# In chains of seven products, ScalarE copies one more partial sum out of PSUM, VectorE's lower add moves behind the fourth product, and the last due steps take no weight splits

## The chip, the cores and the metric

The kernel runs on one core of a Trainium2 chip. A core has TensorE (PE in the profile, with PEld for its weight loads), VectorE (DVE), ScalarE (ACT), GpSimd (POOL) and SyncE (SP), each with its own instruction stream, and DMA queues; engines wait for each other by semaphores. The metric is the device time of one execution in microseconds (us), the median over several runs.

## The reference

The reference is a decoder trunk of two layers on a sequence of 512 positions and 1024 features, in float32. Layer 0 mixes tokens by dilated sliding-window attention with 24 heads in three groups, layer 1 by a gated linear recurrence; each is followed by a gated FFN with a causal convolution of three taps. Cut to what the change touches:

```python
qkv = (x @ w_qkv).reshape(B, S, N_GROUPS, 3, HEADS_PER_GROUP, HEAD_DIM)

def causal_dwconv(x, w, b):
    K = w.shape[0]
    xp = jnp.pad(x, ((0, 0), (K - 1, 0), (0, 0)))
    out = b
    for k in range(K):
        out = out + xp[:, k:k + S] * w[k]
    return out

def conv_ffn(x, w_up, conv_w, conv_b, w_down):
    u = causal_dwconv(x @ w_up, conv_w, conv_b)
    g, v = u[..., :D_FF], u[..., D_FF:]
    return (jax.nn.gelu(g, approximate=True) * v) @ w_down
```

## The kernel before, in words

**Precision.** Each float32 operand is split into a high and a low part: ScalarE writes `whi` (L220), VectorE subtracts it from the raw value and writes `wlo` (L221). A product is then three passes of TensorE, hi by hi, hi by lo and lo by hi (`PASSES`). The weights come by DMA into `raw`, and for the chains GpSimd's queue adds blocks of them to each other by accumulating DMAs (L257); VectorE forms one of the sums itself (L283).

**Chains.** The first projection of both FFNs and the q and k projections of two head groups are done in chains: two 256-row halves of the weights by two 256-column halves of the activations in seven products instead of eight, with sums and differences of weight blocks (`LEFT`) and of activation blocks (`T`). One product is 12 matmuls of 128x256 (4 blocks by 3 passes, L1184). A chain uses two PSUM banks of 128x512. In `y[1]`, the left half gathers products 1, 6, 7 and 4 one upon another. In `y[0]`, the right half gathers products 5 and 3, and the left half is product 2. Two SBUF tiles `t[0]` and `t[1]` (named `part`) take copies by ScalarE: product 1, the sum of 1 and 6, and product 5 (L1193). After product 3, VectorE adds `t[0]` to `y[0]`, which completes the chain's upper result (L1197), and calls `top`. After product 7, VectorE writes the right half of `y[1]`, the sum of 1, 6 and 7 plus the copy of 5 (L1202); after product 4 the bank is the lower result, and `bottom` is called.

There are 56 chains: 16 in attention (`quad` weights) and 20 in each FFN (function `seven`, for `j` in 2 to 11, two halves each). In attention, `top` and `bottom` are one VectorE multiply each, from the bank to SBUF. In an FFN they are `begin`: ScalarE writes `u` from the whole bank with one tap's weight and the bias (L885; for lower results with negated weights, `neg`), VectorE adds the two other taps (L889, two instructions), then ScalarE applies gelu (L909) or VectorE multiplies with the gate (L913).

**What sets the order.** The order is written out by hand, and each engine works through its own list. `steps` gives each product a number: in an FFN chain `n` starts at 10 n (`CYCLE`) with its products at the offsets `AT` (1: 0, 5: 1, 2: 2, 6: 4, 3: 5, 7: 8, 4: 13), so that product 4 runs in the middle of the next chain; free numbers are filled with the second projection (`acc` matmuls, L493). TensorE's order in the middle of the stage is so 1, 5, 2, 4 of the chain before, 6, 3, fill, fill, 7. `slot` runs a step, then the functions that came due (`later(1, f)`: behind the next step), then `tick`, which pumps weight splits: at most `HALVES` = 14 split halves may be live. While `state["hold"]` is set, `tick` pumps none. Behind the last numbered step `seven` empties the list of due functions, one slot each.

Of the kernel before, what the change touches and what calls it, by code (L numbers as in the profile page):

```python
# [14 lines left out]
AF = mybir.ActivationFunctionType  # L15
ALU = mybir.AluOpType
# [118 lines left out]
def kernel(  # L135
# [25 lines left out]
    nc = tc.nc  # L161
# [19 lines left out]
    def nm(s):  # L181
        uid[0] += 1
        return f"{s}{uid[0]}"
# [18 lines left out]
    def new_last():  # L202
        return up_.tile([P, 2 * D + EVEN], F32R, tag="sum", name=nm("last"))
# [15 lines left out]
    def split(hi, lo, raw):  # L219
        nc.scalar.activation(hi, raw, AF.Copy)  # L220
        nc.vector.tensor_tensor(lo, raw, hi.bitcast(F32), op=ALU.subtract)  # L221

    plan = []
    state = {"dma": 0, "cv": 0, "used": 0, "live": 0, "next": 0, "hold": False, "even": False, "quiet": False, "still": False}
# [122 lines left out]
    def refill():  # L347

        i = state["cv"]
        if i >= state["dma"]:  # L350
            return
        if plan[i][0] == "quad":
            pieces.extend(strided_stream(i))
            state["cv"] += 24
            return
        if plan[i][0] == "seven":
            n = 1
            while plan[i + n][0] == "seven":
                n += 1
            pieces.extend(stream(i, n))  # L360
            state["cv"] += n
        else:
            if plan[i + 1 : i + 2] and plan[i + 1][0] == "seven":
                pieces.append((None, lambda: ahead(i + 1)))
            parts = parts_of(plan[i][0], raws[i])
            pieces.extend(plain(i, j, r, j == len(parts) - 1) for j, r in enumerate(parts))
            state["cv"] += 1

    def beside(key):
        return plan[key[0]][4:] and key[1] == 1  # L370

    def single(name):
        return (name[0] if isinstance(name, tuple) else name) in HALF

    def pump(limit=2):

        for _ in range(limit):
            if not pieces:
                refill()
            while pieces and pieces[0][0] is None:  # L380
                pieces.pop(0)[1]()
            if not pieces or pieces[0][0][0] >= state["dma"]:
                continue
            spare = beside(pieces[0][0])
            if spare and state["even"]:
                continue
            if spare or state["live"] + 2 - single(pieces[0][0][1]) <= HALVES:
                key, cuts, last = pieces.pop(0)
                cuts = cuts()
                his, los = [], []  # L390
                if spare:
                    t = new_last()[:, EVEN:].rearrange("p (a b o c) -> p a b o c", a=2, b=2, o=1)
                for n, raw in enumerate(cuts):
                    if spare:
                        hi, lo = t[:, 0, n], t[:, 1, n]
                    else:
                        hi, lo = (
                            wp.tile([P] + list(raw.shape[1:]), F32R, tag=t, name=nm("w" + t)) for t in ("hi", "lo")
                        )
                    split(hi, lo, raw)  # L400
                    his.append(hi)
                    los.append(lo)
                units[key] = (his, los)
                state["live"] += len(cuts) * (not spare)
                state["used"] += last
                while pieces and pieces[0][0] is None:
                    pieces.pop(0)[1]()
            while not state["quiet"] and state["dma"] < len(plan) and state["dma"] - state["used"] < RAW_BUFS:
                load()

    def load():
        i = state["dma"]
        kind, kd, cols, srcs = plan[i][:4]
        raw = wp.tile([P, kd, cols], F32, tag="raw", name=nm("raw"), bufs=RAW_BUFS)
        at = 0
        for src, n in srcs:
            nc.sync.dma_start(raw[:, :, at : at + n] if kind == "value" else raw[:, at : at + n, :], src)
            at += n
        raws[i] = raw
        state["dma"] += 1  # L420
# [13 lines left out]
    def done(n=2):  # L434
        state["live"] -= n
# [6 lines left out]
    def later(n, f):  # L442
        due.append([n, f])

    def slot(emit, length=1):
        emit()
        for d in list(due):
            d[0] -= 1
            if d[0] < 0:
                due.remove(d)  # L450
                d[1]()
        tick(length)
# [4 lines left out]
    def tick(length=1):  # L457
        for s in list(sides):
            s[0] -= length
            if s[0] <= 0:  # L460
                try:
                    s[0] = next(s[1])
                except StopIteration:
                    sides.remove(s)
        if not (state["hold"] or state["still"]):
            pump(1 if state["even"] or state["live"] >= HALVES - 4 else 2)
# [704 lines left out]
    def chain(right, top, bottom):  # L1171

        i = chunk()
        y, t = {}, []

        def step(n):
            W = take(i, LEFT[n][0])
            b, at = {1: (1, 0), 6: (1, 0), 7: (1, 0), 4: (1, 0), 5: (0, 256), 3: (0, 256), 2: (0, 0)}[n]
            if b not in y:
                y[b] = psum()  # L1180
            dst = y[b][:, at : at + 256]
            for k in range(4):
                for q, (wa, ha) in enumerate(PASSES):
                    mm(  # L1184
                        dst, W[wa][0][:, k, :], right[n](ha, k), start=n in (1, 5) and k == q == 0,
                        stop=k == 3 and q == 2, skip_group_check=True,
                    )
            done(1)
            if n == 1:
                t.extend(gen(s="part") for _ in range(2))  # L1190
            if n in (1, 5, 6):
                to = {1: t[0][:, 0:256], 6: t[0][:, 256:512], 5: t[1][:, 0:256]}[n]
                later(1, lambda: nc.scalar.activation(to, dst, AF.Copy))  # L1193
            elif n == 3:

                def upper():
                    nc.vector.tensor_tensor(y[0], y[0], t[0], op=ALU.add)  # L1197
                    top(y[0])

                later(1, upper)  # L1200
            elif n == 7:
                later(1, lambda: nc.vector.tensor_tensor(y[1][:, 256:512], dst, t[1][:, 0:256], op=ALU.add))  # L1202
            elif n == 4:
                later(1, lambda: bottom(y[1]))

        return lambda n: lambda: step(n)

    def seven(hT, T, begin, last, prep):

        right = rights(hT, T)  # L1210
        i0, acc, ends_at = state["next"], {}, CYCLE * 2 * len(SEVEN)

        def finish(b, ps, j, minus=False):
            later(2, begin(b, ps, j, minus, True))

        def ends(j, half):
            return (
                lambda ps: later(0, lambda: finish(2 * half, ps, j)),
                lambda ps: finish(2 * half + 1, ps, j, True),
            )  # L1220

        def rows(k, pair):
            W, A = take(i0, ("rows", k)), take(i0, ("act", k))
            for t in pair:
                if t not in acc:
                    acc[t] = psum("acc")
                mm3(acc[t], [a[0][:, of_tile(t)] for a in A], [two(w[0]) for w in W], not k, False)
            if pair[-1] == 3:
                done(2)

        fill = quarters(last, 1, hT, lambda ps: finish(3, ps, SEVEN[0] - 1))
        fill += [lambda k=k, p=p: rows(k, p) for k in range(REST[0]) for p in ((0, 1), (2, 3))]
        steps = {}
        n = 0
        for j in SEVEN:
            for half in range(2):
                f = chain(right, *ends(j, half))
                steps.update((CYCLE * n + AT[p], f(p)) for p in AT)
                n += 1
        free = free_slots(n)  # L1240
        assert len(free) == len(fill)
        steps.update(zip(free, fill))
        state["even"] = True
        for m in range(max(steps) + 1):
            if m == ends_at + 1:
                prep()
            if m in steps:
                slot(steps[m])
                if m > 2 * CYCLE and m % 5 == 0 and state["live"] < HALVES - 2:
                    pump(1)  # L1250
        while due:
            slot(lambda: None)
        state["even"] = False
        return acc

# [622 lines left out]
```

## Time and profile before

| | |
|---|---|
| median of 3 runs | 1365.1 us (1363.44 to 1367.1) |
| profiled execution | 1369.2 us, span 1367.4 us |
| PE busy over the span | 1338.2 us (98%) |
| VectorE busy over the span | 1103.7 us (81%) |
| ScalarE busy over the span | 807.7 us (59%) |
| first FFN's middle, 557 to 749 us | PE 192.00, VectorE 170.06, ScalarE 128.66 of 192 us |
| second FFN's middle, 1077 to 1269 us | PE 192.00, VectorE 170.05, ScalarE 128.76 of 192 us |
| attention's chains, 150 to 444 us | PE 287.69, VectorE 236.59, ScalarE 152.21 of 294 us |

A row of a timeline gives the start and the length in us, the engine, the line, the operation, output<-input by the program's names, the shape and the count of a run of like instructions, and in brackets the time that the engine was idle before it and what ended this. A row of a group gives line, engine, operation, names and count, then busy us, mean ns of one, and idle time before with its releaser.

### The profile page before, as it was taken

Reading aid. Unit: us, or ns where it says so; the run is one execution under the profiler, and the core shown is the slowest. Engines: PE = TensorE matmul, PEld = TensorE weight load, DVE = VectorE, ACT = ScalarE, POOL = GpSimd, SP = SyncE. Lnnn points to the kernel's source line nnn. Section 1 sums busy time; section 2 is a strip of 40 time slices with the busy share of each in tenths; the row PEclk is TensorE's granted clock in tenths of the full one; section 3 lists DMA queues with packets and bytes.
Section 4 is the critical chain, followed back from the end, with each engine's and each line's share of the span. In section 5 each row is a group of like instructions: output and inputs, shape, how many; then the busy total and the mean of one; then the engine's idle time right before and its main releaser. Section 6 shows DMA issues by size and latency. Waiting matters only on the chain.

```text
span 1367.4 us, 24126 instructions
## 1 busy us (share of the span) xinstructions
PE 1338.2 (98%) x8981; PEld 1255.3 (92%) x8981; DVE 1103.7 (81%) x2173; ACT 807.7 (59%) x1690; POOL 236.4 (17%) x392
## 2 busy tenths in 40 slices
PE   9999999999999999999999999999999999999997
PEld 7888999889899999999999889978899999999996
DVE  6686888887876899988888759768899988888853
ACT  7343555454546476666666646489576667666641
POOL 0341341212120102221221002000102222221000
PEclk9999999999999999999999999999999999999999
DMA  7553454747483647777775542431446777776411
GB/s 231 184 148 123 124 188 122 214 109 227 120 243 99 263 155 155 183 179 175 169 169 146 174 164 81 151 109 54 162 149 148 178 182 181 178 181 163 165 68 62
DMA packets 70638, 214.53 MB, mean 157 GB/s; under 512 B 10816, under 2 KB 14360, under 8 KB 58744
## 3 DMA queue, kind: packets, MB, share of 16 engines
q1 hardware_dynamic: 42552, 153.34, 33.2%
q0 software_dynamic: 27120, 58.60, 21.2%
q8 instruction: 70, 1.15, 0.3%
q10 hardware_dynamic: 848, 1.05, 0.2%
q14 instruction: 48, 0.39, 0.1%
HBM read 193.99 MB, written 18.96 MB: 156 GB/s over the span
## 4 chain that ended last, share of the span: by engine, by line
PE 62%; issue 19%; DVE 11%; DMA 5%; ACT 3%; POOL 0%; DVEq 0%; POOLq 0%; ACTq 0%; SPq 0%
PE ps L1184 31%; PE acc L493 16%; PE ps L493 6%; PE v L1381 6%; DVE wlo L221 4%; DMA raw<-in_attn_w_qkv_dram 2%; DVE u L889 1%; DMA raw<-in_ffn_w_up_dram 1%; PE v L1319 1%; PE S L1527 1%; ACT whi L220 1%; DMA ft<-turned 1%; PE S L1475 1%; PE O L493 1%; DVE ps L1197 0%
## 5 line engine op out<-in xcount | busy, mean ns | idle before, releaser
L221 DVE TENSOR_TENSOR wlo<-raw,whi 128x512 fp32r<-128x512 f32 x628 | 417.4, 686 | 94.8 <-ACT whi L220 94.1
L220 ACT ACTIVATE whi<-raw 128x512 fp32r<-128x512 f32 x628 | 370.8, 624 | 153.1 <-PE acc L493 43.5
L1184 PE MATMUL ps<-T,whi 128*128 128x256 f32 x1344 | 235.6, 276 | 0.3
L1184 PE MATMUL ps<-hT,whi 128*128 128x256 f32 x1344 | 235.0, 276 | 0.0
L493 PE MATMUL ps<-hT,whi 128*128 128x512 f32 (+1 forms) x928 | 223.8, 334 | 0.2 <-ACT whi L220 0.2
L1184 PEld LDWEIGHTS ps<-T,whi 128*128 128x128 f32 x1344 | 207.4, 191 | 2.9 <-ACT part L1193 0.7
L1184 PEld LDWEIGHTS ps<-hT,whi 128*128 128x128 f32 x1344 | 204.3, 191 | 0.7 <-ACT part L1193 0.2
L1184 PE MATMUL ps<-T,wlo 128*128 128x256 f32 x672 | 185.3, 276 | 0.0
L1184 PE MATMUL ps<-hT,wlo 128*128 128x256 f32 x672 | 185.1, 275 | 0.0
L493 PEld LDWEIGHTS ps<-hT,whi 128*128 128x128 f32 x928 | 159.7, 190 | 13.9 <-ACT whi L220 0.4
L257 POOL DMA_DIRECT2D raw<-in_ffn_w_up_dram x120 | 104.2, 950 | 391.8 <-DVE wlo L221 308.8
L493 PE MATMUL ps<-hT,wlo 128*128 128x512 f32 (+1 forms) x464 | 154.3, 333 | 0.4 <-DVE wlo L221 0.4
L493 PE MATMUL acc<-whi,ahi 128*128 128x512 f32 x336 | 128.0, 381 | 1.8 <-DVE u L889 1.8
L493 PE MATMUL acc<-whi,alo 128*128 128x512 f32 x336 | 127.7, 380 | 1.7 <-DVE alo L221 1.6
L1184 PEld LDWEIGHTS ps<-T,wlo 128*128 128x128 f32 x672 | 128.2, 191 | 0.0
L1184 PEld LDWEIGHTS ps<-hT,wlo 128*128 128x128 f32 x672 | 128.2, 191 | 0.0
L493 PE MATMUL acc<-wlo,ahi 128*128 128x512 f32 x336 | 127.3, 379 | 0.0
L1193 ACT ACTIVATE part<-ps 128x256 f32<-128x256 f32 x168 | 63.9, 380 | 76.7 <-PE ps L1184 73.9
L1381 PE MATMUL v<-whi,hT 128*128 128x512 f32 x320 | 102.7, 384 | 0.0
L493 PEld LDWEIGHTS ps<-hT,wlo 128*128 128x128 f32 x464 | 88.3, 190 | 7.5 <-DVE wlo L221 0.6
L1184 PE MATMUL ps<-last,whi 128*128 128x256 f32 x448 | 79.5, 278 | 6.5 <-DVE ps L1202 6.5
L889 DVE SCALAR_TENSOR_TENSOR u<-ps,cols,u 128x511 f32<-128x511 f32 x112 | 83.5, 746 | 2.0
(227 smaller groups left out, 2453.3 us busy)
## 6 DMA issues: line engine op xcount, KB each, us to landing
raw<-in_ffn_w_up_dram SPq DMA_DIRECT2D x48, 1024.0 KB
raw<-in_attn_w_qkv_dram SPq DMA_DIRECT2D x34, 1024.0 KB
raw<-in_ffn_w_up_dram POOLq DMA_DIRECT2D x120, 256.0 KB, 5.6
raw<-in_ffn_w_down_dram SPq DMA_DIRECT2D x14, 1024.0 KB
dw<-in_ffn_w_down_dram SPq DMA_DIRECT2D x40, 256.0 KB
raw<-in_lru_w_in_dram SPq DMA_DIRECT2D x8, 1024.0 KB
turned<-T POOLq DMA_DIRECT2D x26, 256.0 KB, 2.6
ft<-turned POOLq DMA_DIRECT2D x104, 64.0 KB, 4.9
```

The lines of the kernel that those rows point to most:

```text
L220: nc.scalar.activation(hi, raw, AF.Copy)
L221: nc.vector.tensor_tensor(lo, raw, hi.bitcast(F32), op=ALU.subtract)
L257: nc.gpsimd.dma_start(blocks(i)[to], plan[i][3][0][0][:, 4 * b : 4 * b + 4, :], accum_op=ALU.add)
L493: mm(dst, l[a], r[b], start=start and n == 0, stop=stop and n == 2)
L889: nc.vector.scalar_tensor_tensor(u[:, d:], ps[:, : S - d], wc, u[:, d:], op0=ALU.mult, op1=ALU.add)
L1184: mm(dst, W[wa][0][:, k, :], right[n](ha, k), start=n in (1, 5) and k == q == 0, stop=k == 3 and q == 2, skip_group_check=True,)
L1193: later(1, lambda: nc.scalar.activation(to, dst, AF.Copy))
L1319: mm(banks[t], hT[a][:, k, t * P : (t + 1) * P], two(W[b][k % 2][:, 0, :]), start=u == n == 0, stop=u == 3 and n == 5,)
L1381: mm(bank, hT[a][:, k, t * P : (t + 1) * P], two(W[b][k % 2][:, 0, :]), start=(k, a, b) == (0, 0, 0), stop=(k, a, b) == (KD - 1, 1, 0),)
L1475: mm(Sp[a // 2][:, o + lo : o + 256], q[hh][:, a * P : (a + 1) * P], k[hh][:, k0 : (a + 1) * P], start=True, stop=True)
L1527: mm(ps[:, c], q[hh][:, c], k[hh][:, c], start=True, stop=True)
```

## The change

After product 7 VectorE no longer adds; ScalarE copies the sum of 1, 6 and 7 to the right half of `t[1]`, which was unused. After product 4 VectorE adds the two halves of `t[1]` into the right half of `y[1]`, directly ahead of `bottom`. And `hold` is set while `seven` empties its list of due functions.

```diff
             elif n == 7:
-                later(1, lambda: nc.vector.tensor_tensor(y[1][:, 256:512], dst, t[1][:, 0:256], op=ALU.add))
+                later(1, lambda: nc.scalar.activation(t[1][:, 256:512], dst, AF.Copy))
             elif n == 4:
-                later(1, lambda: bottom(y[1]))
+
+                def lower():
+                    nc.vector.tensor_tensor(y[1][:, 256:512], t[1][:, 256:512], t[1][:, 0:256], op=ALU.add)
+                    bottom(y[1])
+
+                later(1, lower)
...
+        state["hold"] = True
         while due:
             slot(lambda: None)
+        state["hold"] = False
         state["even"] = False
```

In the changed kernel L1202 is ScalarE's copy and L1206 VectorE's add. TensorE's, SyncE's and GpSimd's lists are the same in both. VectorE has 2144 rows in both; ScalarE has 56 more, one copy a chain. In the rows below a name carries a number that tells tiles apart, and the numbers differ between the two kernels.

First place: VectorE, middle of the first FFN, from the upper half's last tap to the lower half's taps, one chain. Before:

```order
L889 SCALAR_TENSOR_TENSOR u_8038<-ps_7926,cols_1214,u_8038 128x510
L221 TENSOR_TENSOR wlo_8059<-raw_7585,whi_8058 128x512
L1202 TENSOR_TENSOR ps_7905<-ps_7905,part_7919 128x256
L221 TENSOR_TENSOR wlo_8081<-raw_7903,whi_8080 128x512
L221 TENSOR_TENSOR wlo_8101<-raw_7744,whi_8100 128x512
L221 TENSOR_TENSOR wlo_8118<-dw_7870,whi_8117 128x512
L221 TENSOR_TENSOR wlo_8134<-u_7514,whi_8133 128x512
L283 TENSOR_TENSOR raw_7744<-raw_7744 128x512
L221 TENSOR_TENSOR wlo_8153<-raw_7903,whi_8152 128x512
L889 SCALAR_TENSOR_TENSOR u_8150<-ps_7905,neg_5821,u_8150 128x511
L889 SCALAR_TENSOR_TENSOR u_8150<-ps_7905,neg_5821,u_8150 128x510
```

Changed:

```order
L889 SCALAR_TENSOR_TENSOR u_8064<-ps_7951,cols_1214,u_8064 128x510
L221 TENSOR_TENSOR wlo_8085<-raw_7608,whi_8084 128x512
L221 TENSOR_TENSOR wlo_8107<-raw_7928,whi_8106 128x512
L221 TENSOR_TENSOR wlo_8127<-raw_7768,whi_8126 128x512
L221 TENSOR_TENSOR wlo_8144<-dw_7895,whi_8143 128x512
L221 TENSOR_TENSOR wlo_8160<-u_7537,whi_8159 128x512
L283 TENSOR_TENSOR raw_7768<-raw_7768 128x512
L1206 TENSOR_TENSOR ps_7930<-part_7944 128x256
L221 TENSOR_TENSOR wlo_8180<-raw_7928,whi_8179 128x512
L889 SCALAR_TENSOR_TENSOR u_8177<-ps_7930,neg_5837,u_8177 128x511
L889 SCALAR_TENSOR_TENSOR u_8177<-ps_7930,neg_5837,u_8177 128x510
```

The add has moved back past four splits and L283, to one split ahead of the taps of its own bank.

Second place: ScalarE, the same stage, one stretch of a chain, with the semaphores that each row waits for. Before:

```order
L220 ACTIVATE whi_7921<-raw_7744 128x512 [waits DMAHW0_49,PE_49]
L1193 ACTIVATE part_7918<-ps_7905 128x256 [waits PE_49]
L220 ACTIVATE whi_7941<-raw_7585 128x512 [waits DMASW1_49]
L1193 ACTIVATE part_7919<-ps_7926 128x256 [waits PE_49]
L220 ACTIVATE whi_7958<-dw_7711 128x512 [waits DMAHW7_49]
L220 ACTIVATE whi_7974<-u_7402 128x512
L885 ACTIVATE u_7991<-ps_7746,cols_1218,neg_5821 128x512 [waits DVE_49,PE_49]
L220 ACTIVATE whi_7993<-raw_7744 128x512 [waits DMASW2_49]
L1193 ACTIVATE part_7918<-ps_7905 128x256 [waits PE_49]
```

Changed:

```order
L1202 ACTIVATE part_7784<-ps_7770 128x256 [waits PE_49]
L220 ACTIVATE whi_7946<-raw_7768 128x512 [waits DMAHW0_49]
L1193 ACTIVATE part_7943<-ps_7930 128x256 [waits PE_49]
L220 ACTIVATE whi_7966<-raw_7608 128x512 [waits DMASW1_49]
L1193 ACTIVATE part_7944<-ps_7951 128x256 [waits PE_49]
L220 ACTIVATE whi_7983<-dw_7735 128x512 [waits DMAHW7_49]
L220 ACTIVATE whi_7999<-u_7424 128x512
L885 ACTIVATE u_8017<-ps_7770,cols_1218,neg_5837 128x512 [waits DVE_49]
L220 ACTIVATE whi_8019<-raw_7768 128x512 [waits DMASW2_49]
L1193 ACTIVATE part_7943<-ps_7930 128x256 [waits PE_49]
```

The new copy stands at the head of the stretch; the rest keeps its order. L885 (`neg`) stands ahead of a split and of the copy of the sum of 1 and 6 in both; in the changed kernel its wait is for VectorE alone. The `whi` behind L885 is the one whose `wlo` VectorE has directly behind L1206.

Third place: VectorE at the end of the second FFN's chains. Before:

```order
L1202 TENSOR_TENSOR ps_15401<-ps_15401,part_15415 128x256
L221 TENSOR_TENSOR alo_15560<-u_12092,ahi_15559 128x512
L221 TENSOR_TENSOR alo_15564<-u_12131,ahi_15563 128x512
L913 TENSOR_TENSOR u_15371<-u_15371,u_15528 128x512
L221 TENSOR_TENSOR wlo_15575<-raw_15377,whi_15574 128x512
L221 TENSOR_TENSOR wlo_15579<-raw_15377,whi_15578 128x512
L221 TENSOR_TENSOR wlo_15597<-raw_15440,whi_15596 128x512
L221 TENSOR_TENSOR wlo_15601<-raw_15440,whi_15600 128x512
L889 SCALAR_TENSOR_TENSOR u_15604<-ps_15401,neg_11888,u_15604 128x511
L889 SCALAR_TENSOR_TENSOR u_15604<-ps_15401,neg_11888,u_15604 128x510
L913 TENSOR_TENSOR u_15487<-u_15487,u_15604 128x512
```

Changed:

```order
L221 TENSOR_TENSOR alo_15615<-u_12128,ahi_15614 128x512
L221 TENSOR_TENSOR alo_15619<-u_12167,ahi_15618 128x512
L913 TENSOR_TENSOR u_15425<-u_15425,u_15583 128x512
L221 TENSOR_TENSOR wlo_15630<-raw_15431,whi_15629 128x512
L221 TENSOR_TENSOR wlo_15634<-raw_15431,whi_15633 128x512
L221 TENSOR_TENSOR wlo_15652<-raw_15494,whi_15651 128x512
L221 TENSOR_TENSOR wlo_15656<-raw_15494,whi_15655 128x512
L1206 TENSOR_TENSOR ps_15455<-part_15469 128x256
L889 SCALAR_TENSOR_TENSOR u_15660<-ps_15455,neg_11924,u_15660 128x511
L889 SCALAR_TENSOR_TENSOR u_15660<-ps_15455,neg_11924,u_15660 128x510
L913 TENSOR_TENSOR u_15542<-u_15542,u_15660 128x512
```

The add has moved to directly ahead of the last taps; the four splits ahead of the taps stand there in both, and with `hold` left out of the changed kernel every list is the same.

## The prediction

> **What bounds the kernel now.** First the page's span and busy shares, then the chain of work that ended last, then busy time by stage. The profiled execution took 1369.2 us around its span, 4.1 us more than the median of the runs shown (1365.1); the sum below is made on 1369.2 and 4.1 is taken off at the end.
>
> ```profile
> span 1367.4 us, 24126 instructions
> PE 1338.2 (98%) x8981; PEld 1255.3 (92%) x8981; DVE 1103.7 (81%) x2173; ACT 807.7 (59%) x1690; POOL 236.4 (17%) x392
> ```
>
> TensorE is busy 98% of the span. The chain of waits, in order of time (start, length, what), runs along TensorE through the middle of the first FFN, one chain of seven products after another, and gives their period: 9.38 + 2.60 = 11.98 us.
>
> ```profile
> 605.05 9.38 PE ps L1184 x84
> 614.43 2.60 PE acc L493 x12
> ```
>
> Busy time by stage (start:end, length, then busy us with the number of instructions of PE, PEld, DVE, ACT, POOL; granted clock; DMA share; GB/s), first for 16 chains of the first FFN's middle, then for the attention stage that holds the 16 chains there:
>
> ```profile
> 557.00:749.00 192.00, 192.00 (x1541) 188.16 (x1540) 170.06 (x274) 128.66 (x241) 38.24 (x44) 1.00 0.70 172
> 150.00:444.00 294.00, 287.69 (x2114) 274.83 (x2113) 236.59 (x564) 152.21 (x391) 71.43 (x131) 1.00 0.55 164
> ```
>
> In the FFN TensorE never stops and sets the time, but VectorE is close behind it: 170.06 / 16 = 10.63 us of work in a period of 11.98, so 1.35 us idle a chain. ScalarE has 128.66 / 16 = 8.04 and is far from its limit. What the change may add to VectorE's 11.98 before TensorE has to wait is therefore the question. VectorE's timeline over one period (start, length, line, what; in brackets idle time before and who ended it):
>
> ```profile
> 611.38 0.69 DVE L221 TENSOR_TENSOR wlo<-dw,whi 128x512 fp32r<-128x512 f32 x1 [1.09 <-ACT whi L220]
> 611.99 0.69 DVE L221 TENSOR_TENSOR wlo<-u,whi 128x512 fp32r<-128x512 f32 x1
> 612.60 0.68 DVE L283 TENSOR_TENSOR raw<-raw 128x512 f32<-128x512 f32 x1
> 613.20 0.68 DVE L221 TENSOR_TENSOR wlo<-raw,whi 128x512 fp32r<-128x512 f32 x1
> 613.80 1.53 DVE L889 SCALAR_TENSOR_TENSOR u<-ps,neg,u 128x511 f32<-128x511 f32 x2
> ...
> 615.84 0.69 DVE L1197 TENSOR_TENSOR ps<-ps,part 128x512 f32<-128x512 f32 x1
> ...
> 617.90 0.69 DVE L221 TENSOR_TENSOR wlo<-raw,whi 128x512 fp32r<-128x512 f32 x1 [0.77 <-ACT whi L220]
> 618.51 1.53 DVE L889 SCALAR_TENSOR_TENSOR u<-ps,cols,u 128x511 f32<-128x511 f32 x2
> ...
> 620.55 0.43 DVE L1202 TENSOR_TENSOR ps<-ps,part 128x256 f32<-128x256 f32 x1
> 620.89 0.68 DVE L221 TENSOR_TENSOR wlo<-raw,whi 128x512 fp32r<-128x512 f32 x1
> ...
> 623.36 0.69 DVE L221 TENSOR_TENSOR wlo<-dw,whi 128x512 fp32r<-128x512 f32 x1 [0.59 <-ACT whi L220]
> ```
>
> and ScalarE's, in the same period:
>
> ```profile
> 611.79 0.79 ACT L885 ACTIVATE u<-ps,cols,neg 128x512 f32<-128x512 f32 x1
> 612.47 0.61 ACT L220 ACTIVATE whi<-raw 128x512 fp32r<-128x512 f32 x1
> 613.13 0.39 ACT L1193 ACTIVATE part<-ps 128x256 f32<-128x256 f32 x1
> ...
> 616.57 0.78 ACT L885 ACTIVATE u<-ps,cols 128x512 f32<-128x512 f32 x1 [0.52 <-DVE ps L1197]
> ```
>
> Two things are to be seen. The upper half already shows the pattern that the change will give the lower one: L1197 (VectorE), then L885 (ScalarE), then the split that ScalarE queues behind L885, whose low part VectorE waits for: 0.77 us idle at 617.90, with one older split in between. In the lower half no such wait stands: L885 starts at 611.79, long before VectorE's L283 and wlo. And the other idle time is soft: VectorE has caught up and waits for ScalarE's high part of a dw weight. The groups of the same 16 chains (busy us, mean ns; idle before, releaser) give its size and the prices:
>
> ```profile
> L1197 DVE TENSOR_TENSOR ps<-ps,part 128x512 f32<-128x512 f32 x17 | 11.8, 692 | 0.0
> L221 DVE TENSOR_TENSOR wlo<-dw,whi 128x512 fp32r<-128x512 f32 x17 | 11.8, 691 | 12.4 <-ACT whi L220 12.4
> L283 DVE TENSOR_TENSOR raw<-raw 128x512 f32<-128x512 f32 x16 | 10.9, 684 | 0.0
> L1202 DVE TENSOR_TENSOR ps<-ps,part 128x256 f32<-128x256 f32 x16 | 6.8, 426 | 0.0
> ```
>
> 12.4 / 16 = 0.78 us a chain is soft; what VectorE truly needs for a chain is 11.98 - 0.78 = 11.20.
>
> **The change part by part. The FFN chains (40 of 56).** The add is the same size as before and there are as many of them; it moves from behind product 7 to behind product 4, directly ahead of the bottom half's L885. L885 reads the whole bank, so it now waits for the add (L1206), and L1206 stands on VectorE behind L283 and ahead of the wlo whose whi ScalarE has queued behind L885. In the timeline above: L283 starts at 612.60, the next instruction at 613.20; that is now L1206. From its start to the start of the next split: 0.43 (L1202's length) + 0.04 hand-over (L1197 starts 615.84, ends 616.53, L885 at 616.57) + 0.68 (L885 at 611.79 to whi at 612.47) + 0.61 (that whi) + 0.04 = 1.80 us. Before, the split stood at 613.20 at once; the old add took 620.89 - 620.55 = 0.34 elsewhere. Net +1.46 us a chain, nearly all of it a bubble on VectorE (0.04 + 0.68 + 0.61 + 0.04 = 1.37): L889, the taps, stand behind the split, so nothing fills it.
>
> VectorE then needs 11.20 + 1.46 = 12.66 us against 11.98: 0.68 too much a chain. Bounds: were all 1.35 of idle time soft, 10.63 + 1.46 - 11.98 = 0.11 too much; were only half of the 0.78 soft (the gelu and the next whi on ScalarE come later too), 0.68 + 0.39 = 1.07. I take 0.68, because the 0.77 in the upper half is set by VectorE's own L1197 and moves along with it.
>
> Who waits then: ScalarE's copies behind the late L885. The copy of product 6 at 613.13 starts 613.67 - 611.79 = 1.88 us later (613.67 = 613.20 + 0.43 + 0.04). Product 7 accumulates on that copy's source; its first matmul:
>
> ```profile
> 616.87 0.38 PE L1184 MATMUL ps<-T,whi 128*128 128x256 f32 x2
> ```
>
> Its spare is 616.87 - 613.52 = 3.35 us, so 1.5 us are left, used up after two or three chains; from there TensorE runs at VectorE's pace. A stage of 20 chains costs 20 x 0.68 - 1.5 = 12.1 us; two stages **+24.2**.
>
> **Product 4's waits go.** Its first matmul no longer waits for VectorE's add but for ScalarE's copy. The page's group of its first pass (busy us, mean ns; idle before, releaser):
>
> ```profile
> L1184 PE MATMUL ps<-last,whi 128*128 128x256 f32 x448 | 79.5, 278 | 6.5 <-DVE ps L1202 6.5
> ```
>
> and these 6.5 us one by one in TensorE's timeline:
>
> ```profile
> 182.65 0.50 PE L1184 MATMUL ps<-last,whi 128*128 128x256 f32 x2 [0.60 <-DVE ps L1202]
> 275.06 0.50 PE L1184 MATMUL ps<-last,whi 128*128 128x256 f32 x2 [2.01 <-DVE ps L1202]
> 343.83 0.50 PE L1184 MATMUL ps<-last,whi 128*128 128x256 f32 x2 [1.26 <-DVE ps L1202]
> 550.25 0.49 PE L1184 MATMUL ps<-last,whi 128*128 128x256 f32 x2 [1.41 <-DVE ps L1202]
> 1069.98 0.49 PE L1184 MATMUL ps<-last,whi 128*128 128x256 f32 x2 [1.19 <-DVE ps L1202]
> ```
>
> ScalarE's timeline shortly ahead of the first two:
>
> ```profile
> 180.78 0.39 ACT L1193 ACTIVATE part<-ps 128x256 f32<-128x256 f32 x1 [1.63 <-PE ps L1184]
> 272.44 1.28 ACT L220 ACTIVATE whi<-raw 128x512 fp32r<-128x512 f32 x2 [2.72 <-PE v L1381]
> ```
>
> The first three lie in attention, where ScalarE stands idle at these places (1.63 and 2.72 us), so the copy comes at once: **-3.87** (bounds: 0, if the add merely stalls VectorE later there, to -3.87). The next two lie at the start of each FFN: **-2.60** (bounds 0 to -2.60). In attention the consumer of the bottom is VectorE's own multiply, behind the add on the same engine: no hand-over, no bubble; 236.59 busy of 294.00 hides the shift.
>
> **The ends of both FFN stages.** There TensorE waits today for the last taps, so what delays them costs in full:
>
> ```profile
> 770.41 0.46 PE L493 MATMUL acc<-whi,ahi 128*128 128x512 f32 x1 [0.89 <-DVE u L889]
> 1290.15 0.46 PE L493 MATMUL acc<-whi,ahi 128*128 128x512 f32 x1 [0.89 <-DVE u L889]
> ```
>
> The second of these ends on VectorE and ScalarE:
>
> ```profile
> 1286.07 2.49 DVE L221 TENSOR_TENSOR wlo<-raw,whi 128x512 fp32r<-128x512 f32 x4
> 1286.48 0.76 ACT L885 ACTIVATE u<-ps,cols,neg 128x512 f32<-128x512 f32 x1
> 1288.47 1.53 DVE L889 SCALAR_TENSOR_TENSOR u<-ps,neg,u 128x511 f32<-128x511 f32 x2
> ```
>
> L885 at 1286.48 ran under four splits; now L1206 comes behind the splits, L885 behind L1206 and the taps behind L885: 0.43 + 0.04 + 0.76 + 0.04 = 1.27 each, up to 1.27 + 1.5 = 2.8 if VectorE also arrives late by the spare that the stage used up. I take 2.0, the middle: **+4.0** (bounds 2.5 to 5.6).
>
> **The copies** are 56 more ScalarE instructions of about 0.38 us (the copy at 613.13 took 0.39): 8.42 of 11.98 a chain, hidden. Uncovered they would cost 56 x 0.38 = 21 us. **The hold** (no splits among the last due steps): no split is issued in those steps before either; every split stands where it stood, so 0 (were it to free the last taps of the four splits ahead of them, at most the 0.89 that TensorE waits at each end, -1.8).
>
> [...]
>
> Sum: 24.2 + 4.0 - 3.87 - 2.60 = +21.7; 1369.2 + 21.7 = 1390.9 on the profiled execution, 1390.9 - 4.1 = **1387** against the median. With 0.40 to 0.95 a chain, this case's own range is 1376 to 1398.
>
> **The rivals.** *The bubble fits* (it decides if VectorE loses no more than its idle time, 1.35 with all of it soft, and product 7's spare spread over a stage, 1.5 / 20 = 0.08). For it: 1.46 against 1.43 is close; against it: of the 1.35 only the 0.78 is a wait that a late VectorE skips, since the 0.77 at 617.90 moves along with L1197. Then -3.87 - 2.60 + 2 x 1.27 = -3.9, 1361; with ends that cost nothing, 1359. Chance 0.12, half of it beyond the bound. *Break-even*: 0.15 too much a chain, 2 x (3.0 - 1.5) + 4.0 - 6.5 = +0.5, 1366; chance 0.04. *Half is absorbed*: were it ready weights and not copies that TensorE runs out of, a stage would live on the splits made ahead for longer; with half the loss 12.1 + 4.0 - 6.5 = +9.6, 1375; against it, that ScalarE's copies stand in one queue with L885 and product 7 has only 3.35 to spare. Chance 0.07. *The chase gets worse*: 1.07 too much, because ScalarE, itself late, hands the dw and gelu later to VectorE: 2 x (21.4 - 1.5) + 4.0 - 6.5 = +37.3, 1402; chance 0.09. *The hold does nothing* holds with 0.95 within any of these and moves none.
>
> **How the numbers follow.** The forecast has 0.68. About 0.3% (4.1 us) is what a measurement of this kernel can tell from no change. Slower: 0.68 + 0.07 + 0.09 = 0.84; same: 0.04 + 0.06 = 0.10; faster: 0.06. The range reaches from the first rival to the chase, 1361 to 1403, and leaves out about half of the first and a third of the chase.
>
> **What would show it.** Right: the period in the middle of each FFN near 12.66 instead of 11.98; VectorE idle about 1.4 us ahead of the wlo behind L1206, released by ScalarE's whi; ScalarE's L885 (neg) waiting for L1206 where its group shows 0.0 now or none; product 7 waiting for ScalarE's copy; no wait of product 4 on VectorE; attention 4 us shorter. Wrong: a period still at 11.98 with VectorE's waits for dw gone, which would mean that more than 0.78 was soft.

## The result, and the profile after

The changed kernel takes 1401.0 us (median of four runs, 1400.2 to 1402.0) against 1365.3 before: a ratio of 1.0264, 95% interval 1.0249 to 1.0279, so 35.7 us slower. The sign, the place and the mechanism are those of the forecast (1387, range 1361 to 1403); the size lies next to that of its rival in which the chase gets worse (1402), but is made up of other terms, as shown below. The profiled execution took 1400.2 us. The page's span and busy shares of the changed kernel:

```profile
span 1398.4 us, 24157 instructions
PE 1349.5 (96%) x8981; PEld 1256.0 (90%) x8981; DVE 1107.5 (79%) x2173; ACT 811.4 (58%) x1746; POOL 237.0 (17%) x392
```

VectorE and ScalarE are busy under 4 us longer each. TensorE, whose list is the same, stands idle for 1398.4 - 1349.5 = 48.9 us where it was 29.2, and part of its own 11.3 us more is a slower clock (0.995 granted over the span where it was 0.997, see below). The chain of work that ended last, in order of time, over two chains of seven products in the middle of the first FFN:

```profile
606.86 2.94 PE ps L1184 x24
609.80 2.60 PE acc L493 x12
612.40 6.71 PE ps L1184 x60
620.32 1.89 DVE wlo L221 x3
...
632.42 2.94 PE ps L1184 x24
```

Before, this path stayed on TensorE. Now it goes from TensorE to VectorE and back, and two chains take 632.42 - 606.86 = 25.56 us, 12.78 each where it was 11.98. VectorE's timeline shows why:

```profile
607.36 0.69 DVE L221 TENSOR_TENSOR wlo<-raw,whi 128x512 fp32r<-128x512 f32 x1 [0.36 <-ACT whi L220]
...
609.36 0.69 DVE L283 TENSOR_TENSOR raw<-raw 128x512 f32<-128x512 f32 x1
609.96 0.43 DVE L1206 TENSOR_TENSOR ps<-part 128x256 f32<-128x256 f32 x1
611.75 0.69 DVE L221 TENSOR_TENSOR wlo<-raw,whi 128x512 fp32r<-128x512 f32 x1 [1.37 <-ACT whi L220]
612.36 1.53 DVE L889 SCALAR_TENSOR_TENSOR u<-ps,neg,u 128x511 f32<-128x511 f32 x2
...
616.46 0.69 DVE L221 TENSOR_TENSOR wlo<-raw,whi 128x512 fp32r<-128x512 f32 x1 [0.78 <-ACT whi L220]
```

and ScalarE's, what it does in the bubble:

```profile
605.90 0.63 ACT L909 ACTIVATE u<-u 128x512 f32<-128x512 f32 x1 [0.96 <-DVE u L889]
606.44 0.37 ACT L1193 ACTIVATE part<-ps 128x256 f32<-128x256 f32 x1
606.70 0.63 ACT L220 ACTIVATE whi<-raw 128x512 fp32r<-128x512 f32 x1
...
610.42 0.78 ACT L885 ACTIVATE u<-ps,cols,neg 128x512 f32<-128x512 f32 x1 [1.79 <-DVE ps L1206]
611.10 0.62 ACT L220 ACTIVATE whi<-raw 128x512 fp32r<-128x512 f32 x1
611.62 0.37 ACT L1193 ACTIVATE part<-ps 128x256 f32<-128x256 f32 x1
```

Behind L1206 VectorE is idle for 1.37 us, until L885 and the whi queued behind it are done; the wait of 0.78 us behind L1197 is still there; and the soft waits for dw weights are gone. First the group of L885 before, then four groups of the changed kernel, each over 16 periods (557.00 to 749.00 us before, to 761.50 us after):

```profile
L885 ACT ACTIVATE u<-ps,cols,neg 128x512 f32<-128x512 f32 x16 | 12.6, 787 | 0.0
...
L885 ACT ACTIVATE u<-ps,cols,neg 128x512 f32<-128x512 f32 x16 | 12.5, 778 | 39.5 <-DVE ps L1206 39.5
L221 DVE TENSOR_TENSOR wlo<-dw,whi 128x512 fp32r<-128x512 f32 x17 | 11.7, 689 | 0.9
L221 DVE TENSOR_TENSOR wlo<-raw,whi 128x512 fp32r<-128x512 f32 x111 | 74.8, 687 | 32.2 <-ACT whi L220 32.2
L1184 PE MATMUL ps<-T,whi 128*128 128x256 f32 x384 | 68.4, 279 | 7.9 <-ACT part L1193 7.9
```

L885 of the lower results waits 39.5 / 16 = 2.5 us for the add, where it waited for nothing before. Before dw VectorE waited 12.4 us over such a stretch; now 0.9. And TensorE's wait is for ScalarE's copies (L1193). In every second chain the one waited for stands behind L885 and its whi (611.62 in the timeline is such a copy), in the others behind the gelu of L909 (606.44), which waits for VectorE's taps.

The ends of the FFN stages, on TensorE (timeline), and the window behind (in it the granted clock is the number behind POOL's):

```profile
772.72 0.49 PE L493 MATMUL acc<-whi,alo 128*128 128x512 f32 x1 [0.54 <-DVE alo L221]
779.20 0.46 PE L493 MATMUL acc<-whi,ahi 128*128 128x512 f32 x1 [3.40 <-DVE u L889]
```

```profile
780.00:783.40 3.40, 3.40 (x10) 2.69 (x9) 1.72 (x4) 1.42 (x3) 0.00 (x0) 0.51 0.02 5
```

The wait for the last taps has grown from 0.89 to 3.40 us, and from 780.06, 0.9 us behind it, TensorE runs at half rate for 3.4 us. Behind the 0.89 the granted clock stayed at 1.00 (770.40 to 774.00 us). The second FFN's end shows the same 3.40 (to 1319.84 us) and a half rate of the same length (0.50 from 1319.36 to 1322.77 us).

In the group of all 56 chains product 4 has no wait for VectorE any more; what is left is mostly a wait of 0.45 us for ScalarE's copy at the end of each FFN:

```profile
L1184 PE MATMUL ps<-last,whi 128*128 128x256 f32 x448 | 79.1, 277 | 1.1 <-ACT part L1202 0.9
```

**Where the 35.7 us lie.** TensorE's list is the same in both kernels, so its instructions can be laid side by side, one by one. From the first to the last chain matmul an FFN stage takes 262.0 us where it took 247.1 (both stages alike): +29.7 for two, of it -2.6 for the two starting waits that went. The two ends cost 5.0 and 4.8: +9.8. Product 4's three waits in attention are not there: -0.8, -2.2 and -1.4 = -4.4. The rest, some -4 us on balance, lies mostly in the profiled execution of before: in its first 30 us it was 1.9 us later, and at one product of attention 2.1 and 0.7 us later than the changed kernel, the first time for a DMA:

```profile
260.09 1.13 PE L1593 MATMUL O<-ft,vp 128*128 128x128 f32 x8 [1.85 <-DMA toe<-rowv]
```

No later trace shows this wait, not that of the kernel before with an added copy either, whose median is that of before and whose profiled span is 4.3 us shorter. That trace and that of the early add, below, lack the third of product 4's waits too (343.83, 1.26 us), though their adds stand ahead of product 4. So this wait does not hang on the place of the add alone, and only the first two, -3.0, can be put down to the change.

### The profile page after: what moved, and what is told of

Its sections match the earlier page's. It is cut to its first block, busy times and chain, and to the rows that moved or that the text cites. A ratio compares the mean times of both kernels' runs of the same rounds, so it can differ in the third digit from the quotient of the medians.

```text
span 1398.4 us, 24157 instructions
## 1 busy us (share of the span) xinstructions
PE 1349.5 (96%) x8981; PEld 1256.0 (90%) x8981; DVE 1107.5 (79%) x2173; ACT 811.4 (58%) x1746; POOL 237.0 (17%) x392
## 4 chain that ended last, share of the span: by engine, by line
PE 49%; issue 20%; DVE 19%; ACT 6%; POOL 4%; DMA 1%; DVEq 0%; POOLq 0%; SPq 0%; ACTq 0%
PE ps L1184 15%; PE acc L493 13%; PE ps L493 7%; PE v L1388 7%; DVE wlo L221 6%; POOL raw L257 4%; DVE u L889 3%; ACT whi L220 2%; DVE xb L1693 1%; PE S L1534 1%; PE O L1600 1%; PE v L1326 1%; DVE x_sb L690 1%; PE S L1482 1%; DMA raw<-in_ffn_w_up_dram 1%
## 5 line engine op out<-in xcount | busy, mean ns | idle before, releaser
L1184 PE MATMUL ps<-T,whi 128*128 128x256 f32 x1344 | 239.7, 279 | 20.9 <-ACT part L1193 20.6
L885 ACT ACTIVATE u<-ps,cols,neg 128x512 f32<-128x512 f32 x40 | 31.1, 778 | 101.5 <-DVE ps L1206 101.5
L547 POOL DMA_DIRECT2D ft<-turned x136 | 74.8, 557 | 34.8 <-DMA ft<-turned 7.4
```

Of the source, the lines that this page charges most:

```text
L547: nc.gpsimd.dma_start(t[32 * c : 32 * c + 32].rearrange("j (b x) -> j b x", b=4), d.rearrange("(b j) (c x) -> c j b x", j=32, c=4)[c],)
L885: nc.scalar.activation(u, ps, AF.Identity, scale=own[:, j : j + 1], bias=cc[:, 48 + j : 49 + j])
L1184: mm(dst, W[wa][0][:, k, :], right[n](ha, k), start=n in (1, 5) and k == q == 0, stop=k == 3 and q == 2, skip_group_check=True,)
```

## The experiments

All ratios are against runs of the kernel before on the same chip: 1365.4 us in the first four, 1364.2 on another chip in the last four. Differences from the change's 1401.0 us are between medians of different rounds, whose kernels before differ by about 1 us.

| kernel | median, us | ratio, 95% interval |
|---|---|---|
| early add | 1374.1 | 1.0059, 1.0037 to 1.0080 |
| extra copy | 1364.8 | 0.9997, 0.9981 to 1.0012 |
| attention alone | 1359.8 | 0.9958, 0.9943 to 0.9972 |
| L885 one step later | 1365.0 | 0.9990, 0.9977 to 1.0004 |
| one tap left out | 1367.3 | 1.0014, 0.9995 to 1.0034 |
| hold that acts | 1392.7 | 1.0199, 1.0168 to 1.0231 |
| attention alone, hold that acts | 1358.4 | 0.9941, 0.9920 to 0.9962 |
| L885 one step later, hold that acts | 1357.1 | 0.9935, 0.9912 to 0.9958 |

**Do the copies themselves cost?** The kernel before, with the copy added:

```diff
             elif n == 7:
+                later(1, lambda: nc.scalar.activation(t[1][:, 256:512], dst, AF.Copy))
                 later(1, lambda: nc.vector.tensor_tensor(y[1][:, 256:512], dst, t[1][:, 0:256], op=ALU.add))
```

> The kernel before, with ScalarE's copy after product 7 added in all 56 chains; nothing reads it, and VectorE adds from PSUM as before. Bubble theory: the copies are hidden, 1363 to 1369 us (product 4 waits for whichever of the two readers is later, so none of the waits goes). Copy theory: 1385 us or more.

1364.8 us, no difference. In its window of the FFN's middle TensorE is busy throughout, with ScalarE at 134.34 of 192 us:

```profile
557.00:749.00 192.00, 192.00 (x1542) 188.14 (x1541) 170.01 (x274) 134.34 (x259) 38.24 (x44) 1.00 0.69 171
```

The copy theory falls; the 56 copies are hidden.

**Does the place of the add alone make the loss?** The copy stays, the add comes one step behind it, ahead of product 4:

```diff
             elif n == 7:
-                later(1, lambda: nc.vector.tensor_tensor(y[1][:, 256:512], dst, t[1][:, 0:256], op=ALU.add))
+                later(1, lambda: nc.scalar.activation(t[1][:, 256:512], dst, AF.Copy))
+                later(2, lambda: nc.vector.tensor_tensor(y[1][:, 256:512], t[1][:, 256:512], t[1][:, 0:256], op=ALU.add))
```

> ScalarE's copy after product 7 stays, in all 56 chains, but VectorE adds the two SBUF halves one step after the copy, ahead of product 4, not directly ahead of the bottom half; the order around the due steps at the end is that of before. Bubble theory (the loss is VectorE's idle 1.37 us a chain between the add and the split whose high part ScalarE has queued behind L885): no bubble, period back at 11.98 us (12.78 in the changed kernel), product 4's waits for VectorE gone (3.9 to 7 us in attention, 2.6 in the FFNs), ends as before: 1355 to 1360 us. Copy theory (56 more ScalarE copies make ScalarE late, and TensorE waits for its copies): the copies are all there, so 1390 us or more.

1374.1 us: both numbers were wrong. In the FFN's middle TensorE is busy throughout and VectorE no longer idles behind the add, so the bubble is gone with the late add, as expected. The period, by the starts of the same matmul twelve chains apart, is 12.06 us, not quite 11.98:

```profile
557.00:749.00 192.00, 192.00 (x1530) 187.38 (x1529) 169.17 (x271) 134.50 (x256) 38.24 (x44) 1.00 0.68 169
```

But product 4's waits for VectorE did not go. They grew, as the group of all 56 chains shows, in the extra copy and then here, and one wait at the start of an FFN in the timeline:

```profile
L1184 PE MATMUL ps<-last,whi 128*128 128x256 f32 x448 | 79.5, 278 | 5.6 <-DVE ps L1203 5.6
...
L1184 PE MATMUL ps<-last,whi 128*128 128x256 f32 x448 | 80.9, 281 | 11.1 <-DVE ps L1203 10.8 <-ACT whi L220 0.3
```

```profile
547.04 0.46 PE L1184 MATMUL ps<-last,whi 128*128 128x256 f32 x2 [2.23 <-DVE ps L1203]
```

The add no longer reads what product 4 writes, only SBUF, and writes the other half of the bank. Still product 4 waits for it, 10.8 us in all; the one thing that the two share is the bank. So it is not the copy that freed product 4 in the change, but that VectorE has no access to the bank left ahead of it; the copy only makes this possible. A step later on VectorE, the add is later than the old one was. Of the +8.7 us, 5.5 are these waits (11.1 where the extra copy has 5.6), and about 1.7 is a slower clock behind the same wait of 2.23 us at the start of the second FFN (granted 0.79 over the 8 us from 1068 to 1076, so 8 x 0.21); shorter waits of product 4 inside the stages, which make the period 12.06, are the rest, less what the ends gain. What would happen without product 4's wait for the add no run here shows.

**Is it the order behind the add?** In the changed kernel, the lower result's L885 comes one step behind the add, as the upper one's does behind L1197:

```diff
-                lambda ps: finish(2 * half + 1, ps, j, True),
+                lambda ps: later(0, lambda: finish(2 * half + 1, ps, j, True)),
```

> The changed kernel, but in the FFNs L885 of a lower result comes one step behind the add, as that of an upper result does: ScalarE's next split and its copy of the sum of 1 and 6 stand ahead of L885, and VectorE has a split behind the add, L1197 ahead of the taps, and the lower taps behind L1197. Bubble theory: of the 1.37 us about 0.76 stays and the 0.2 to 0.8 us behind L1197 is filled by the taps, need 11.7 to 12.0 us, period 11.98; what is left are the ends (+1.3 to +2.5 each) against attention's gain: 1358 to 1368 us. A theory in which the add behind product 4 itself is too late for the next chain's banks: the lower bank comes free another step later, 1401 us or more.

1365.0 us, as expected. The add, the copy and their waits are those of the change; only ScalarE's next split and its copy of the sum of 1 and 6 now stand ahead of L885. VectorE's timeline, and the window of 16 chains:

```profile
616.51 0.43 DVE L1206 TENSOR_TENSOR ps<-part 128x256 f32<-128x256 f32 x1
616.85 0.69 DVE L221 TENSOR_TENSOR wlo<-raw,whi 128x512 fp32r<-128x512 f32 x1
618.30 0.69 DVE L221 TENSOR_TENSOR wlo<-raw,whi 128x512 fp32r<-128x512 f32 x1 [0.77 <-ACT whi L220]
618.91 0.69 DVE L1197 TENSOR_TENSOR ps<-ps,part 128x512 f32<-128x512 f32 x1
```

```profile
557.00:749.00 192.00, 192.00 (x1541) 188.23 (x1540) 170.27 (x274) 132.30 (x257) 37.23 (x43) 1.00 0.70 172
```

0.77 of the 1.37 us is left and the period is 11.98 again. That the add behind product 4 is itself too late for the banks falls. What this kernel gains in attention it loses at the ends, where TensorE waits for the last taps:

```profile
763.16 0.77 PE L493 MATMUL acc<-whi,ahi 128*128 128x512 f32 x1 [2.50 <-DVE u L889]
```

**Is the period VectorE's work, or a loop of waits?** The changed kernel with one VectorE tap a chain left out:

```diff
-                for d, wc in ((1, near[:, 48 + j : 49 + j]), (2, far[:, j : j + 1])):
+                for d, wc in ((1, near[:, 48 + j : 49 + j]), (2, far[:, j : j + 1]))[: 1 if minus else 2]:
```

> The changed kernel with the second of the two L889 taps of the lower results left out (40 VectorE instructions of about 0.75 us; the convolution lacks that tap there, so this is only a test of time); every wait, the bubble behind L1206 included, stays as it is. VectorE-bound theory (period = VectorE's work + its hard waits, 12.78 us): 12.78 - 0.75 = 12.03, the period falls to about 12.0 and the stages lose almost nothing; the ends are 0.75 us less late each: 1366 to 1372 us. Latency theory (the period is the loop product 4, L1206, L885, the split, the copy of the sum of 1 and 6, product 7, and VectorE's amount of work does not matter): the tap is not in that loop, 1396 to 1401 us.

1367.3 us: 33.7 less than the change for 40 x 0.75 = 30 us of VectorE work; and the clock granted over the span is 0.997 where the change has 0.995, worth some 2.8 us (an estimate, 0.002 x 1398). The chain of its trace lies on TensorE again, at 11.98 us:

```profile
609.24 9.38 PE ps L1184 x84
618.62 2.60 PE acc L493 x12
621.22 9.40 PE ps L1184 x84
```

The bubble and every wait that the latency theory rests on are still in this kernel. So the period is set by VectorE's work and its bubbles together, and the latency theory falls.

**The ends.** The hold as the change places it moves no instruction. Set earlier, it takes four splits from ahead of the last add:

```diff
+            if m == max(steps) - 2:
+                state["hold"] = True
             if m in steps:
                 slot(steps[m])
```

> The changed kernel, with the hold set three steps before the last step instead of behind it, so that the four splits ahead of the last L1206 of each FFN move behind the last taps. If the end's loss is the add that stands behind these four splits, TensorE's last wait for the taps falls from 3.40 us by four splits of 0.60 to about 1.0, and with it the slow clock behind it (3.3 us at half rate, 1.7 us each): 2 x (2.4 + 1.7) = -8, 1390 to 1395 us. If the splits then come too late for the next products, the same time is lost there: 1399 to 1403 us.

1392.7 us, 8.3 less than the change, as expected. TensorE's waits for the taps, in the changed kernel (total, times, longest)

```profile
PE acc L493 <- DVE u L889: 6.8, 2, 3.4
```

and with the earlier hold:

```profile
PE acc L493 <- DVE u L889: 1.9, 2, 0.9
```

The clock granted over this kernel's span is 0.997 where the changed kernel has 0.995, and the period in the middle is still 12.78 us.

**What is worth keeping.** The change in attention alone (FFN chains built with `late=False`):

```diff
             elif n == 7:
+                if late:
+                    later(1, lambda: nc.scalar.activation(t[1][:, 256:512], dst, AF.Copy))
+                else:
+                    later(1, lambda: nc.vector.tensor_tensor(y[1][:, 256:512], dst, t[1][:, 0:256], op=ALU.add))
...
-                f = chain(right, *ends(j, half))
+                f = chain(right, *ends(j, half), late=False)
```

> The change in the 16 attention chains alone; the 40 FFN chains add as before (the hold is in). Bubble theory: in attention the consumer of the lower result is VectorE itself, so only product 4's waits go, by the prediction -3.9 us, by the two profiles up to -7.5: 1358 to 1362 us. If the copies themselves cost: 16/56 of the loss, 1375 us.

1359.8 us, 5.6 less than before. With the earlier hold beside it:

> The change in the 16 attention chains alone, FFN chains as before, and the hold set three steps before the last as well, so that the last taps of each FFN no longer stand behind four splits. TensorE's 0.89 us waits for the last taps go, -1.8 us against the kernel with the change in attention alone (1359.8): 1357 to 1359 us. If the four splits come too late afterwards: 1360 to 1364 us.

1358.4 us: on the chip of its runs 5.8 less than before, so the further gain is of the expected sign but smaller than the runs can tell. And L885 one step later in all chains, with the earlier hold:

> L885 of the lower results one step behind the add, as in the run above that brought the changed kernel back to 1365, and the hold set three steps before the last. That run kept the gain of attention and lost about 4.5 us at each end (TensorE idle 2.7 us, then about 3.4 us at half rate). With four splits out of the way the idle time falls under 1 us and the clock should stay up: 1365 - 2 x (1.8 + 1.7) = 1358 us; 1363 to 1366 us if the end's loss is not the splits.

1357.1 us, 7.1 less than before, the fastest of all; against the 1358.4 of the kernel that leaves the FFNs alone the runs tell no difference. So the late add is worth its gain in attention, and in the FFNs, once its bubble is filled and the ends are cleared, nothing that these runs can tell.

## Why the prediction was right, and by how much it missed

- *VectorE is close behind TensorE and a bubble on it becomes period*: right. The 1.37 us worked out from L885, whi and two hand-overs was measured as 1.37 in chain after chain; removing it (L885 one step later) or removing as much work elsewhere (one tap) brought back 11.98.
- *12.66 us of need, 0.68 too much*: mis-sized. Measured 12.78, 0.80 too much. The missing 0.12 lies in the term that the range named and the sum left at nothing, gelu and the next whi on ScalarE coming later: the row at 607.36 waits 0.36 us in every second chain, behind a gelu that itself waited 0.96 for the taps. That is 0.18 a chain, a little more than is missing.
- *A stage costs 20 x 0.68 - 1.5 = 12.1*: about 16.2 apart from its starting wait. 2.4 of the difference is the period; the other 1.7 is about the spare that was to be used up first and in effect was not there. It was read in the middle of the stage; at the stage's start product 4 waited for VectorE already. In the changed kernel TensorE waits 1.01 us for a copy (535.11) already 26 us into the stage. That this is the reason is argued, not tried.
- *Product 7 waits for the copy of 1 and 6*: half right. It does so in every second chain, and in the others product 6 waits for the copy of 1 (606.86).
- *Attention -3.87*: right in what goes and near in size: -4.4 by the instructions side by side, -5.6 (3.8 to 7.8) by the runs. But the third of its three waits, 1.26, is not in the traces of two kernels whose adds stand ahead of product 4. It most likely belonged to the profiled execution alone, for which the sum takes 4.1 off besides; then it was counted twice.
- *Product 4 "no longer waits for VectorE's add but for ScalarE's copy"*: true of the change, but the copy is only half of the reason: the early add shows that a VectorE write to the other half of the bank ahead of it holds it up just as well (10.8 us in all).
- *Ends +4.0*: mis-sized, the largest miss for its size: +9.8. The taps are 2.5 us later, near the upper bound of 2.8; to this comes 0.5 us of waiting for alo, and the half rate, about 1.7 us each, which no row of before contained at such a place.
- *Copies hidden, hold at nothing*: right; the first by the extra copy, the second by the order, which the hold leaves as it is. The add's reading SBUF in place of PSUM saved nothing: its mean is 426 ns in both kernels.

The terms by what they measured: 29.7 + 9.8 - 4.4 = +35.1, against 35.7 by the medians. That the total is near the rival's 1402 is chance: the rival had 1.07 too much a chain and cheap ends, where 0.80 and dear ends were measured.

## What to carry to other kernels

Before moving an instruction of a nearly full engine ahead of another engine's consumer, look at what that consumer's queue holds behind it and what the first engine needs from there: the price is the whole round trip, here 1.37 us for an instruction of 0.43, and it counts once the full engine's idle time that is a mere wait for others is used up. Such a round trip is filled by letting the consumer come one step later, behind the work that the first engine wants next: 1365.0 us here in place of 1401.0. And a wait of TensorE at a stage's end may cost more than its length, as here the 3.40 us with 3.41 us at half rate behind them, about 1.7 us more.

## What the runs showed of the hardware

In the traces of the kernel before and of the changed kernel the granted clock is 1.0 or 0.5. Between 30 and 1350 us it falls to 0.5 for 3.41 us at a time: once in the kernel before, from 904.90, and three times in the changed one, from 780.06, 967.79 and 1319.36. Matmuls of 128x512 then start every 0.43 us where it is 0.216, so a stretch of 3.41 us that TensorE works through costs about 1.7.

Each of the four lies close to the end of a stall of TensorE. Before, a matmul of the gate starts at 903.96 after 2.86 us of waiting for VectorE, and the half rate begins 0.94 us later. In the changed kernel stalls of 3.40, 2.47 and 3.40 us end at 779.20, 966.47 and 1319.84; the half rate begins 0.86 and 1.32 us behind the first two and 0.48 us ahead of the end of the third.

The length of a stall alone does not decide. The same matmul of the gate waits 2.86 us in the changed kernel too, to 914.43, and there the granted clock stays at 1.00 (908.00 to 960.00 us). In L885 one step later, shorter stalls of 2.50 and 2.49 us at the ends were followed by matmuls 0.43 us apart. What decides was not shown.
